# One level of Strassen on the input products of both feed-forwards, with an output stage of its own

## The chip, the cores and the metric

The kernel runs on one core of one Trainium2 chip. The metric is the device time of one launch in microseconds (us). The core has a matrix engine (TensorE, PE in the rows; its weight loads stand as PEld), a vector engine (VectorE, DVE), a scalar engine (ScalarE, ACT), GpSimd (POOL) and a queue engine (SyncE, SP) that issues the memory transfers (DMA).

## What is computed

Two layers of a streaming encoder on 1024 frames of width 1024. Each has a token mixer and then a SwiGLU feed-forward with 2816 hidden units, each with a norm and a modulation before it and a gated residual add behind it. The change touches the feed-forward alone, with the norm ahead of it:

```python
def swiglu(h, w_in, w_out):
    gate, up = jnp.split(h @ w_in, 2, axis=-1)
    return (jax.nn.silu(gate) * up) @ w_out
...
        h = modulate(rms_norm(x, ln_ffn_g[layer]), sh2, sc2)
        x = x + g2[:, None, :] * swiglu(h, ffn_w_in[layer], ffn_w_out[layer])
```

## The kernel before

Activations lie transposed: the residual `x` is eight tiles of 128 features by 1024 frames, and so is the normed input `HT`. Every large product is made of three matmuls in `mm3` (L246 to L250): each operand is held as a rounded part `hi` and a rest `lo`, and hi·hi, hi·lo and lo·hi are summed in PSUM. One matmul is 128x128 by 128x512.

`Stream` (L100 to L167) brings the weights in a planned order: a transfer of 512 KB into one of four `raw` tiles (L130), a copy to `hi` on ACT (L141) and a subtraction for `lo` on POOL (L142), into one of six `whl` slots. The pump runs at every `pipe.tick`, and generators (`ada`, `norm`, `rms`) advance by ticks too, which is how their work is set among the matmuls. `ada` (L277) is a matrix-vector product of conditioning weights: eight transfers of 512 KB and eight DVE operations (L286, L288).

`out_proj` (L1253) ends the mixer: it adds into `x` (L1266), sums squares (`stat`, L311 and L312), and at its end starts `norm` (L339) for each half of the frames. `norm` takes the row statistic through PE, DVE and POOL (`rms`, L320 to L336) and writes `hi` and `lo` of `HT` (L348 to L351).

`ffn` (L1296) walks over 22 tiles `m` of 128 hidden units. For each `m` and each half of 512 frames it makes a gate and an up product (L1321, 8 blocks of the width, 24 matmuls each), then Silu on ACT (L1326), a product (L1327) and a cast (L1328) on DVE and the rest on POOL (L1329), into `aT`. Every two tiles the output products follow (L1340): 16 groups of 6 matmuls, each added into `x` by DVE (L1342). The first three tiles are done for the first half of the frames before the second half of `HT` is needed. Five calls of `ada` for the next layer are spread over the first five blocks of layer 0. The order on each queue is set when the kernel is built, by a planner that moves an instruction ahead of earlier ones that it holds to be not yet ready.

## Time and profile before

| | us |
|---|---|
| median of 3 runs | 2644.95 (2635.11 to 2645.98) |
| the profiled execution | 2628.13 |
| its span, first to last instruction | 2626.3 |
| PE busy in it | 2535.4 |
| feed-forward of layer 0, about | 580 to 1300 |
| feed-forward of layer 1, about | 1905 to 2623 |

The profile's page gives the busy time of each engine, and the trace can be asked for stretches, groups of instructions, waits and the order in time. A matmul of 128x512 shows 0.39 us in a row because neighbours overlap; what counts is the distance between two starts.

### The profile page before, as it was taken

Reading aid. Unit: us, or ns where it says so; the run is one execution under the profiler, and the core shown is the slowest. Engines: PE = TensorE matmul, PEld = TensorE weight load, DVE = VectorE, ACT = ScalarE, POOL = GpSimd, SP = SyncE. Lnnn points to the kernel's source line nnn. Section 1 sums busy time; section 2 is a strip of 40 time slices with the busy share of each in tenths; the row PEclk is TensorE's granted clock in tenths of the full one; section 3 lists DMA queues with packets and bytes.
Section 4 is the critical chain, followed back from the end, with each engine's and each line's share of the span. In section 5 each row is a group of like instructions: output and inputs, shape, how many; then the busy total and the mean of one; then the engine's idle time right before and its main releaser. Section 6 shows DMA issues by size and latency. Waiting matters only on the chain. (4 is left out here: it accounts for less than half of the span.)

```text
span 2626.3 us, 32531 instructions
## 1 busy us (share of the span) xinstructions
PE 2535.4 (97%) x12912; PEld 2104.9 (80%) x12912; DVE 1134.9 (43%) x2058; ACT 708.9 (27%) x1293; POOL 809.5 (31%) x538
## 2 busy tenths in 40 slices
PE   6999898999999999999999999999999999999999
PEld 4898776777888888888788778887788888888887
DVE  6576563474333322222531566765632222222223
ACT  4332568322111111111232444544231111111100
POOL 3465003423222222232212143423243333333311
PEclk9999999999999999999999999999999999999999
DMA  7287764543233311111234333224311111111101
GB/s 282 92 248 211 211 179 154 184 145 108 93 113 112 113 49 48 48 49 49 87 109 145 87 104 102 68 76 156 112 65 49 49 50 49 50 50 49 49 9 64
DMA packets 145479, 267.12 MB, mean 102 GB/s; under 512 B 34416, under 2 KB 82224, under 8 KB 144560
## 3 DMA queue, kind: packets, MB, share of 16 engines
q1 hardware_dynamic: 145328, 265.05, 31.7%
q8 instruction: 102, 1.67, 0.3%
q14 instruction: 49, 0.40, 0.1%
HBM read 221.22 MB, written 45.88 MB: 102 GB/s over the span
## 5 line engine op out<-in xcount | busy, mean ns | idle before, releaser
L249 PE MATMUL mm<-HT,whl 128*128 128x512 f32 x1744 | 680.3, 390 | 4.5 <-DVE HT L351 4.4
L248 PE MATMUL mm<-HT,whl 128*128 128x512 f32 x1744 | 680.7, 391 | 1.8 <-ACT HT L350 1.5
L250 PE MATMUL mm<-HT,whl 128*128 128x512 f32 x1744 | 679.8, 390 | 0.0
L142 POOL TENSOR_TENSOR whl<-raw,whl 128x1024 fp32r<-128x1024 f32 x136 | 332.5, 2453 | 494.5 <-ACT whl L141 487.8
L249 PEld LDWEIGHTS mm<-HT,whl 128*128 128x128 f32 x1744 | 327.7, 188 | 76.4 <-DVE HT L351 6.7
L248 PEld LDWEIGHTS mm<-HT,whl 128*128 128x128 f32 x1744 | 327.7, 188 | 72.8 <-ACT HT L350 2.8
L250 PEld LDWEIGHTS mm<-HT,whl 128*128 128x128 f32 x1744 | 327.9, 188 | 68.5
L1342 DVE SCALAR_TENSOR_TENSOR x<-at,col,x 128x512 f32<-128x512 f32 x352 | 262.4, 750 | 268.6 <-PE at L250 268.4
L1327 DVE TENSOR_TENSOR sg<-sg,mm 128x512 f32<-128x512 f32 x88 | 60.4, 687 | 642.3 <-PE mm L250 642.3
L249 PE MATMUL at<-aT,wo 128*128 128x512 f32 x704 | 274.9, 390 | 1.9 <-POOL aT L1329 1.9
L250 PE MATMUL at<-aT,wo 128*128 128x512 f32 x704 | 274.8, 390 | 0.0
L248 PE MATMUL at<-aT,wo 128*128 128x512 f32 x704 | 273.1, 391 | 0.0
L248 PE MATMUL mm<-whl,HT 128*128 128x512 f32 (+1 forms) x688 | 249.5, 363 | 8.6 <-ACT HT L402 8.1
L249 PE MATMUL mm<-whl,HT 128*128 128x512 f32 (+1 forms) x688 | 244.8, 356 | 0.0
L142 POOL TENSOR_TENSOR wo<-raw,wo 128x1024 fp32r<-128x1024 f32 x44 | 107.4, 2464 | 442.4 <-ACT wo L141 442.4
L250 PE MATMUL mm<-whl,HT 128*128 128x512 f32 (+1 forms) x688 | 242.1, 357 | 0.0
L141 ACT CAST whl<-raw 128x1024 fp32r<-128x1024 f32 x154 | 161.3, 1054 | 172.3 <-PE mm L250 164.7
L1329 POOL TENSOR_TENSOR aT<-sg,aT 128x512 fp32r<-128x512 f32 x88 | 115.2, 1309 | 289.6 <-DVE aT L1328 281.9
L1326 ACT ACTIVATE sg<-mm 128x512 f32<-128x512 f32 x88 | 52.6, 598 | 518.7 <-PE mm L250 518.7
L141 ACT CAST wo<-raw 128x1024 fp32r<-128x1024 f32 x44 | 44.0, 1046 | 494.2 <-PE at L250 488.0
L248 PEld LDWEIGHTS mm<-whl,HT 128*128 128x128 f32 x688 | 138.0, 201 | 25.7 <-ACT HT L402 10.7
L249 PEld LDWEIGHTS at<-aT,wo 128*128 128x128 f32 x704 | 132.2, 188 | 30.8 <-POOL aT L1329 2.4
(295 smaller groups left out, 3193.0 us busy)
## 6 DMA issues: line engine op xcount, KB each, us to landing
raw<-in_ffn_w_in SPq DMA_DIRECT2D x88, 512.0 KB, 3.5
raw<-in_ada_w SPq DMA_DIRECT2D x80, 512.0 KB, 4.0
raw<-in_ffn_w_out SPq DMA_DIRECT2D x44, 512.0 KB, 3.4
ada<-in_ada SPq DMA_DIRECT2D x16, 512.0 KB, 10.2
qkd<-stk SPq DMA_DIRECT2D x32, 256.0 KB, 4.8
q<-qkd SPq DMA_DIRECT2D x64, 128.0 KB, 3.9
ks<-qkd SPq DMA_DIRECT2D x32, 256.0 KB, 4.3
qkd<-stk SPq DMA_DIRECT2D x16, 512.0 KB, 3.2
```

What stands on the lines that cost most here:

```text
L141: nc.scalar.copy(hi, u.raw[:, :u.n])
L142: self.low.tensor_sub(lo, u.raw[:, :u.n], hi.bitcast(F32))
L248: mm(out, lhs.hi, rhs.hi, start=start, stop=False)
L249: mm(out, lhs.hi, rhs.lo, start=False, stop=False)
L250: mm(out, lhs.lo, rhs.hi, start=False, stop=stop)
L1326: nc.scalar.activation(sg, gu[0], AF.Silu)
L1327: nc.vector.tensor_mul(sg, sg, gu[1])
L1329: nc.gpsimd.tensor_sub(a[m].lo[:, sl], sg, a[m].hi[:, sl].bitcast(F32))
L1342: nc.vector.scalar_tensor_tensor(xh, ps, self.col[layer, 5][:, n:n + 1], xh, M, A)
```

## The change

The weight of a tile `m` is taken as a 2x2 matrix of blocks (gate and up by the first and second half of the width), and the input as a 2x2 matrix (first and second half of the width by first and second half of the frames). Winograd's form of Strassen's scheme gives the four results from seven products of halves, each 4 blocks or 12 matmuls: P1 = A11·B11, P2 = A12·B21, S2·T2, S3·T3, S1·T1, A22·T4 and S4·B22, with sums S of weight blocks and sums T of input blocks.

- `Comb` builds S1 to S4 on DVE from two raw weight tiles and splits each of the seven blocks by an ACT copy and a POOL subtraction of 128x512. `raws` keeps at most two raw tiles outstanding.
- `norm_t` replaces `norm` for the second half of the frames: it forms T1 to T4 from the normed halves and splits each. T1 and B22 go into `HT`, T2 to T4 into twelve tiles `ar`, whose places the residual `x` held; so `x` is first written to memory (`xd`) in `out_proj`.
- `ffn_first` makes P1 and P2 of the first three tiles, from the first half of the frames alone.
- `ffn_in` makes the rest and combines by DVE; the activations (`hi` and `lo`) are written to memory (`ad`), 1 MB for each `m`.
- `ffn_out` is a stage of its own behind it: it loads activations back, eight tiles into `HT` and the last four elsewhere, loads `x` back from `xd`, and makes the output products, in blocks of two tiles and a last one of four. The five `ada` of layer 0 run there, one after another, a tick for every two groups.

```diff
+            some, full = (("S2", "S3"), ("S1", "A22"), ("S4",)), (("A11", "A12"), ("S2", "S3"), ("S1", "A22"), ("S4",))
+            self.win.append([st.pairs(w[m], some if m < EARLY else full, m > 0) for m in range(NH)])
...
+        while self.nd < len(self.units) and self.units[self.nd].ready and (self.units[self.nd].src is None or self.raws() < 2):
...
+class Comb:
...
+        a, b, op = {"S1": ("A21", "A22", A), "S2": ("S1", "A11", S), "S3": ("A11", "A21", S), "S4": ("A12", "S2", S)}[name]
...
+        self.stream.t.nc.vector.tensor_tensor(t, a, b, op)
...
+    def make(self, hl, names):
...
+            nc.scalar.copy(hi, z)
+            nc.gpsimd.tensor_sub(lo, z, hi.bitcast(F32))
...
+    def norm_t(self, pool, fp, ar, x, sb):
...
+        yield 1
+        yield from self.rms(pool, self.acc.pop(1))
...
+        low = [nc.gpsimd, v]
+
+        def put(dst, src):
+            nc.scalar.copy(dst.hi, src)
+            low[0].tensor_sub(dst.lo, src, dst.hi.bitcast(F32))
+            low.reverse()
+
+        for p in range(4):
+            h12, h22 = (pool.tile([P, 512], F32, tag="nf", bufs=3, name="nf") for _ in range(2))
+            for f, k in ((h12, p), (h22, p + 4)):
+                v.scalar_tensor_tensor(f, x[k][:, sl], s[:, k:k + 1], rb, M, M)
+                nc.scalar.activation(f, f, AF.Identity, bias=b[:, k:k + 1])
...
+            v.tensor_sub(t1, h12, b11.hi.bitcast(F32))
+            v.tensor_sub(t1, t1, b11.lo.bitcast(F32))
+            v.tensor_sub(t2, h22, t1)
+            put(self.T[2][p], t2)
+            v.tensor_sub(h12, h22, h12)
+            put(self.T[3][p], h12)
+            put(self.HT[:, p, sl], t1)
+            v.tensor_sub(t4, b21.hi.bitcast(F32), t2)
+            v.tensor_add(t4, t4, b21.lo.bitcast(F32))
+            put(self.T[4][p], t4)
+            put(self.HT[:, p + 4, sl], h22)
+            if p == 1:
+                yield 1
...
+            if h:
+                nc.sync.dma_start(out=self.xd[n], in_=x[n])
...
-                pipe.tick(self.norm(pool, x, h, sb))
+                pipe.tick(second() if h else self.norm(pool, x, h, sb))
...
+    def ffn_first(self, layer, fp):
...
+        for m in range(EARLY):
+            ps = self.mm_bank()
+            self.prod(ps, w[m], [self.HT[:, p, first] for p in range(4)])
...
+            pipe.tick()
+        for m in range(EARLY):
+            ps = self.mm_bank()
+            self.prod(ps, w[m][:, 512:], [self.HT[:, 4 + p, first] for p in range(4)])
+            self.gate(fp, m, self.p1[m], ps)
...
+            pipe.tick()
...
+    def ffn_in(self, layer, fp, tp):
...
+        def put(m, h, src):
+            a = tp.tile([P, 2, 512], F32R, tag="aT", bufs=3, name="aT")
+            nc.scalar.copy(a[:, 0], src)
+            nc.gpsimd.tensor_sub(a[:, 1], src, a[:, 0].bitcast(F32))
+            nc.sync.dma_start(out=self.ad[m][:, :, h * 512:h * 512 + 512], in_=a.bitcast(F32))
...
+            b = self.mm_bank()
+            self.prod(b, w.get("S2"), self.T[2])
+            u = tmp()
+            v.tensor_add(u, self.p1[m], b)
+            pipe.tick()
+            c = self.at_bank()
+            self.prod(c, w.get("S3"), self.T[3])
+            c22 = tmp()
+            v.tensor_add(c22, u, c)
...
+            d = self.at_bank()
+            self.prod(d, w.get("S1"), t1)
+            c21, c22 = c22, tmp()
+            v.tensor_add(c22, c21, d)
+            v.tensor_add(u, u, d)
...
+            e = self.at_bank()
+            self.prod(e, w.get("A22"), self.T[4])
+            v.tensor_add(c21, c21, e)
+            v.tensor_mul(c21, c21, self.sg[m])
+            put(m, 0, c21)
...
+            f = self.at_bank()
+            self.prod(f, w.get("S4"), b22)
+            v.tensor_add(u, u, f)
+            nc.scalar.activation(u, u, AF.Silu)
+            v.tensor_mul(u, u, c22)
+            put(m, 1, u)
...
+    def ffn_out(self, pool, ar, layer, x, done):
...
+                t = self.const.tile([P, 2, T], F32R, tag=f"HT{m % NK}", name="a")
+                nc.sync.dma_start(out=t.bitcast(F32), in_=self.ad[m])
...
+        for m in range(NK):
+            load(m)
...
+        for n in range(NK):
+            nc.sync.dma_start(out=x[n], in_=self.xd[n])
...
+                        self.mm3(ps, wfo[m].k(0)[:, n * P:(n + 1) * P], a[m][h], m == ms[0], m == ms[-1])
...
+                    if n % 2 or last:
                         pipe.tick()
```

## Rows read from the trace of the kernel before

**Rows 1.** Page, part 1: busy time of each engine, share, instructions.

```profile
PE 2535.4 (97%) x12912; PEld 2104.9 (80%) x12912; DVE 1134.9 (43%) x2058; ACT 708.9 (27%) x1293; POOL 809.5 (31%) x538
```

**Rows 2.** Stretches of layer 1's feed-forward: busy us (instructions) of each engine, clock, DMA.

```profile
1950.00:2250.00 300.00, 300.00 (x1321) 247.67 (x1321) 77.13 (x112) 39.84 (x46) 90.97 (x47) 1.00 0.15 51
2250.00:2590.00 340.00, 340.00 (x1497) 280.75 (x1496) 85.48 (x125) 41.42 (x49) 92.93 (x48) 1.00 0.12 38
```

**Rows 3.** PE's waits from 570 to 640 us: us in total, times, longest.

```profile
PE mm L249 <- DVE HT L351: 3.0, 5, 1.4
PE mm L248 <- ACT HT L350: 1.5, 3, 0.7
```

**Rows 4.** Page, part 5: costliest groups; busy us, mean ns, then idle before.

```profile
L1342 DVE SCALAR_TENSOR_TENSOR x<-at,col,x 128x512 f32<-128x512 f32 x352 | 262.4, 750 | 268.6 <-PE at L250 268.4
...
L249 PE MATMUL at<-aT,wo 128*128 128x512 f32 x704 | 274.9, 390 | 1.9 <-POOL aT L1329 1.9
...
L1329 POOL TENSOR_TENSOR aT<-sg,aT 128x512 fp32r<-128x512 f32 x88 | 115.2, 1309 | 289.6 <-DVE aT L1328 281.9
L1326 ACT ACTIVATE sg<-mm 128x512 f32<-128x512 f32 x88 | 52.6, 598 | 518.7 <-PE mm L250 518.7
```

**Rows 5.** DVE from 659 us, output products: start, us, line, idle before.

```profile
660.62 0.75 DVE L1342 SCALAR_TENSOR_TENSOR x<-at,col,x 128x512 f32<-128x512 f32 x1 [0.61 <-PE at L250]
661.98 0.75 DVE L1342 SCALAR_TENSOR_TENSOR x<-at,col,x 128x512 f32<-128x512 f32 x1 [0.61 <-PE at L250]
```

**Rows 6.** Groups of DVE by line and shape, columns as in rows 4.

```profile
L288 DVE SCALAR_TENSOR_TENSOR ada<-raw,scond,ada 128x1024 f32<-128x1024 f32 x70 | 98.0, 1399 | 87.3 <-DMA raw<-in_ada_w 86.9
L1327 DVE TENSOR_TENSOR sg<-sg,mm 128x512 f32<-128x512 f32 x88 | 60.4, 687 | 642.3 <-PE mm L250 642.3
L351 DVE SCALAR_TENSOR_TENSOR HT<-nf,col,HT 128x512 fp32r<-128x512 f32 x48 | 44.4, 952 | 2.3 <-ACT HT L350 1.4
...
L348 DVE SCALAR_TENSOR_TENSOR nf<-x,col,at 128x512 f32<-128x512 f32 x48 | 33.8, 740 | 4.5 <-PE at L336 4.2
```

**Rows 7.** Order in time on DVE, end of layer 1's `out_proj` and after.

```profile
1896.06 2.84 DVE L312 TENSOR_TENSOR acc<-acc,hf 128x512 f32<-128x512 f32 x1
1898.82 5.66 DVE L351 SCALAR_TENSOR_TENSOR HT<-nf,col,HT 128x512 fp32r<-128x512 f32 x2
1904.41 1.39 DVE L348 SCALAR_TENSOR_TENSOR nf<-x,col,at 128x512 f32<-128x512 f32 x2
1905.73 0.74 DVE L1266 SCALAR_TENSOR_TENSOR x<-mm,col,x 128x512 f32<-128x512 f32 x1
...
1914.51 1.76 DVE L330 TENSOR_TENSOR dgt<-ident,ss 128x512 f32<-128x512 f32 x1 [0.90 <-POOL ss L324]
```

**Rows 8.** Order in time on POOL, same stretch.

```profile
1895.94 10.81 POOL L142 TENSOR_TENSOR whl<-raw,whl 128x1024 fp32r<-128x1024 f32 x4 [12.81 <-ACT whl L141]
```

**Rows 9.** Single instructions by line: ns least, median, most; first and last start.

```profile
L351 DVE SCALAR_TENSOR_TENSOR HT<-nf,col,HT x48: 733/747/2890, 558.4 to 1936.7; 128x512 fp32r<-128x512 f32 x48
...
L312 DVE TENSOR_TENSOR acc<-acc,hf x42: 673/686/2889, 490.5 to 1907.9; 128x512 f32<-128x512 f32 x42
...
L1342 DVE SCALAR_TENSOR_TENSOR x<-at,col,x x352: 736/751/752, 644.6 to 2622.6; 128x512 f32<-128x512 f32 x176
```

**Rows 10.** Stretches of 2 us while `x` is loaded, columns as in rows 2.

```profile
484.00:486.00 2.00, 2.00 (x11) 1.65 (x10) 0.34 (x1) 0.00 (x0) 2.00 (x2) 1.00 1.02 418
```

**Rows 11.** Stretches of 2 us with a PE gap, columns as in rows 2.

```profile
1462.00:1464.00 2.00, 0.66 (x2) 0.23 (x2) 1.77 (x2) 2.00 (x6) 0.00 (x0) 0.84 0.32 88
1464.00:1466.00 2.00, 0.00 (x0) 0.00 (x0) 2.00 (x4) 1.26 (x3) 0.00 (x0) 0.50 0.35 99
...
1468.00:1470.00 2.00, 2.00 (x10) 1.78 (x9) 1.90 (x2) 1.34 (x4) 0.68 (x1) 0.50 0.09 27
1470.00:1472.00 2.00, 2.00 (x11) 1.58 (x10) 1.20 (x4) 0.66 (x2) 0.70 (x1) 0.96 0.00 0
```

More of the change, by code (lines that the diff above doesn't have):

```diff
@@ L25 @@
 FB = 2
+EARLY = 3
 EPS = 1e-6
@@ L84, in __init__ @@
         self.ready, self.act = True, None
+        self.make = self.last = None
 class Chunk:
@@ L122, in unit, with pairs @@
         return Chunk(self, [u], n)
+    def pairs(self, src, groups, first):
+        rows = [Unit(src[:, j * 1024:(j + 1) * 1024], 1024, None) for j in range(2)]
+        comb = Comb(self, rows)
+        made = [Unit(None, 1024, "whl") for _ in groups]
+        for u, names in zip(made, groups):
+            u.make = lambda hl, names=names: comb.make(hl, names)
+            for c, name in enumerate(names):
+                comb.at[name] = u, c
+        for r in rows:
+            r.last, r.ready = made[-1], first
+        self.units += rows + made
+        return comb
     def dma(self):
         u = self.units[self.nd]
+        u.issued = self.beat
+        self.nd += 1
+        if u.src is None:
+            return
         u.raw = self.t.raw()
@@ L1250, in cd_phase, with out_proj @@
             pipe.tick()
-    def out_proj(self, pool, layer, x, order, late, sb, extra):
+    def out_proj(self, pool, layer, x, order, late, sb, extra, second):
         nc, pipe = self.nc, self.pipe
@@ new lines, in arm, with prod @@
+    def arm(self, layer, fp):
+        self.stream.pool["sw"] = fp
+        for r in self.win[layer][0].rows:
+            r.ready = True
+    def prod(self, ps, w, rhs, start=True, stop=True):
+        for p in range(4):
+            self.mm3(ps, w[:, p * P:(p + 1) * P], rhs[p], start and p == 0, stop and p == 3)
+    def ffn_first(self, layer, fp):
+        nc, pipe = self.nc, self.pipe
+        first = slice(0, 512)
+        w = [c.k(0) for c in self.wfirst[layer]]
+        self.p1, self.sg = {}, {}
+        for m in range(EARLY):
+            ps = self.mm_bank()
+            self.prod(ps, w[m], [self.HT[:, p, first] for p in range(4)])
+            self.p1[m] = fp.tile([P, 512], F32, tag="p1", bufs=EARLY, name="p1")
+            nc.scalar.copy(self.p1[m], ps)
+            pipe.tick()
[3 more added lines that the diff above has]
+            self.gate(fp, m, self.p1[m], ps)
+            self.wfirst[layer][m].free()
+            pipe.tick()
@@ L1401, in build, with arena, half_layer, run @@
             k.pp = None
-    with tc.tile_pool(name="xp0", bufs=1, reuse_waits="tile") as xp:
-        x = [xp.tile([P, T], F32, name=f"x{n}") for n in range(NK)]
+    def arena(ar):
+        x = {n // 2 + n % 2 * 4: ar.tile([P, T], F32, tag="ar", bufs=12, name="x") for n in range(NK)}
+        return x
+    def half_layer(layer, ar, x, late, before, done, adas=()):
+        with tc.tile_pool(name=f"ph1{layer}", bufs=1, reuse_waits="tile") as fp:
+            with tc.tile_pool(name=f"pre{layer}", bufs=1, reuse_waits="tile") as pre:
+                k.arm(layer, fp)
+                for g in before:
+                    pipe.start(k.ada(pre, layer, g))
+                sb = [(layer, 4), (layer, 3)]
+                tail = k.norm_t(pre, fp, ar, x, sb)
+                ada = k.ada(pre, layer, 5)
+                k.out_proj(pre, layer, x, [0, 1, 2, 4, 5, 6, 7, 3], late, sb, [ada], lambda: tail)
+                k.ffn_first(layer, fp)
+                assert tail.gi_frame is None and ada.gi_frame is None
+            with tc.tile_pool(name=f"at{layer}", bufs=1, reuse_waits="tile") as tp:
+                k.ffn_in(layer, fp, tp)
+        with tc.tile_pool(name=f"ph2{layer}", bufs=1, reuse_waits="tile") as p2:
+            def run():
+                for p in adas:
+                    yield from k.ada(p2, 1, p)
+            pipe.start(run())
+            k.ffn_out(p2, ar, layer, x, lambda n, h: done(p2, n, h))
+            if layer == 0:
+                for t in range(4):
+                    pipe.tick(k.v_tile(p2, "hf", k.wdv, t))
+                    pipe.tick()
+                pipe.drain()
@@ L1435, in build @@
         k.cd_phase(dp, cp)
-    with tc.tile_pool(name="xp1", bufs=1, reuse_waits="tile") as xp:
-        x = [xp.tile([P, T], F32, name=f"x{n}") for n in range(NK)]
+    with tc.tile_pool(name="ar1", bufs=1, reuse_waits="tile") as ar:
+        x = arena(ar)
         for kk in (0, 1, 2, 4, 5, 6):
```

223 lines of the change are left out of this document (128 added, 95 removed).

## Prediction

> **What bounds the kernel now.** The page's first part comes first: PE is busy 97% of the span, no other engine half of it [rows 1]. Busy PE is not yet a bound, so the next view is stretches inside a feed-forward: PE has no idle time in 640 us and the clock is at its full 2.4 GHz [rows 2]. From the same two rows comes the price of a matmul, 640 us / 2818 = 0.227 us from start to start (the 0.39 us of a single row overlaps with its neighbour's). PE's waits around the start of layer 0's feed-forward say what could be missing there: 4.5 us in all for the norm [rows 3]. So in these two stages, 1440 us of the 2628, PE's instruction count times 0.227 us is the time, and anything that takes matmuls away pays in full unless another engine or a transfer becomes late.
>
> **What goes.** Silu runs 88 times, once for each tile and half of both layers [rows 4]; each stands for two products of 24 matmuls, so the input products are 88 x 48 = 4224. Seven products of 12 replace eight: 44 tiles x 84 = 3696. The output products stay 3 x 704 [rows 4]. 528 matmuls x 0.227 = **-120 us**. That a shorter chain of matmuls runs at the same price can be seen already: output groups of six are 1.36 us apart, 0.227 each [rows 5].
>
> **The steady input stage.** A tile now has 84 x 0.227 = 19.1 us of PE. ACT gets seven splits, a copy of P1, two Silu and two activation splits: 12 x 0.60 = 7.2 us [rows 4]. POOL gets seven weight and two activation subtractions of 128x512: 9 x 1.31 = 11.8 us [rows 4]. DVE gets seven operations with one PSUM input, 0.69 each, and six with both inputs in SBUF (four weight sums, two products): 13 x 0.69 = 9.0 us [rows 6]. All are below 19.1 us, but DVE and POOL disturb each other. Where POOL subtracted four weights in a row, at 2.70 us each, DVE operations on two SBUF inputs took 2.8 us instead of 0.69, one for each of POOL's [rows 7, 8]; with PSUM as one input 0.752 us is the most in 352 cases [rows 9]. POOL's operations will be 1.31 us, and one DVE operation beside such a one took 1.76 us [rows 7]. Six at 1.76 and seven at 0.75 make 15.8 us, still below 19.1; weights are asked for more than a tile ahead. I cost this stage at nothing; PE's 19.1 us hide it. The two transfers of activations and two of weights a tile are 2.1 MB in 19.1 us, 110 GB/s, against 418 GB/s seen [rows 10]; nothing again.
>
> **The norm of the second half**, the largest cost. Before, it was 16 DVE operations behind 30 us of PE work on three tiles. `norm_t` has 42 DVE operations: for each of four block pairs two with PSUM (L348's form) and six sums with two SBUF inputs, and 10 of the 20 subtractions for `lo` (34 with two SBUF inputs in all); POOL has the other ten. It can begin when the row statistic is spread. The last evacuation of `out_proj` starts at 1905.73 us and the diagonal is ready at 1914.51 + 1.76, 10.5 us later [rows 7]; the ticks put it behind four products, 4 x 2.72 = 10.9 us; with the small matmuls I take 12 us. On DVE there also stand the four weight sums of tile 1 and two gate sums: 38 operations with two SBUF inputs, ten with PSUM. Their price from both sides: undisturbed (L312's median [rows 9], L348's mean) 38 x 0.69 + 10 x 0.74 = 34 us; at L351's mean of 0.952, which holds POOL's disturbance in the same place [rows 6], 38 x 0.95 + 7.4 = 44 us; with every POOL operation of the stretch (ten, and five for tile 1's weights) paid in full, 34 + 15 x 1.31 = 53 us. I take 44, since L351 is the same work beside the same splits. So the last T is ready 12 + 44 = 56 us after `out_proj`. In that time PE has `ffn_first`, 72 matmuls or 16.3 us, and tile 0's 60, 13.6 us, of which the last quarter waits for the last block pair; parts of tiles 1 and 2 fit only as far as banks and weights go. 56 + 1 - 30 = 27, less 3 for such parts: PE stands 24 us in each layer, **+48 us** (ends: 12 and 45 us a layer, the latter if PE's queue also keeps the order of the program).
>
> The Trainium skill states, in SBUF — State Buffer, section "SBUF: two separate sides", that the port pair that DVE shares with GpSimd is an exclusive lock for a whole instruction, where DVE has two SBUF inputs and GpSimd reads SBUF. By that rule the norm would take the 53 us, which is a rival below. The trace agrees in kind, 2.8 us instead of 0.69, but not to the full sum: POOL's four took 10.81 us and let three DVE operations of 0.7 through in about 8.4 us of it.
>
> **The clock.** After a gap of PE around 1464 us, in which it did next to nothing for two to four us, the granted clock stood at 0.5 (1.2 GHz) from 1464 until about 1470 and then rose [rows 11]. Work in it costs twice: the price here is about 1.5 us of work lost for each long gap, **+3 us** for two.
>
> **From input to output stage.** Output needs 2.1 MB of activations (tiles 0 and 1) and `x`, 4.2 MB. The rate is 418 GB/s [rows 10], so 5 and 10 us. The loads of tiles 0 to 3 wait for `HT` 0 to 3, which the product S1·T1 of the last tile frees, 24 to 36 matmuls (5.4 to 8.2 us) before PE ends; those of 4 to 7 wait for the very last product. The first four output groups go without `x`, 5.4 us, for there are four banks; behind that PE waits for DVE and DVE for `x`. If SP issues `x` ahead of tiles 4 to 7, nothing stands; if behind them (the order of the program), `x` lands about 10 us late. SP's order is the planner's. I take 3 us a layer, **+6 us** (0 and 20).
>
> **`ada` in layer 0's output stage.** Before, one step of it came every 5.4 us, now at every second group, 2.72 us. A whole `ada` is 11 ticks, 30 us of PE. DVE has in that 22 evacuations of 0.75 and eight steps of 1.40 us [rows 6]: 27.7 us, which fits. But DVE stood 86.9 us before 70 steps for their transfers [rows 6], 1.24 us each; with these it is 37.6 us, and evacuations queue behind a waiting step. Five times 7.6 us makes 38 us as the upper end, 0 as the lower one, if the planner lets the steps slide. I take **+10 us**, since four banks take up single waits. Layer 1 has none of it.
>
> Other moves cost nothing as far as rows go: writing `x` out in `out_proj` rides beside 24-matmul groups, and the first half's norm is needed as before. The 4.5 us of old waits may go; I don't count on it.
>
> **Sum.** -120 + 48 + 3 + 6 + 10 = -53 us. On the profiled execution 2628 becomes 2575. The median of the runs shown is 16.8 us above that execution; the same difference gives 2645 - 53 = **2592 us**.
>
> **Rivals.**
> - PE fills the wait: the planner runs ready parts of tiles 1 and 2, DVE goes at its undisturbed price, 12 us a layer, and the rest hides. -120 + 24 + 3: 2552 us. For it: the planner does move matmuls ahead of ones that aren't ready. Against: three DVE operations of the old norm took 2.8 us. Chance 0.20.
> - The shared port lets nothing overlap in `norm_t`: 53 us instead of 44, so some 9 to 11 us more a layer: 2614 us. Chance 0.13.
> - `ada` binds the output stage of layer 0: 38 instead of 10, 2620 us. Chance 0.10.
> - Slower than before: the input stage becomes bound by DVE. The place is DVE's six two-SBUF operations a tile; the point is where they cost more than (19.1 - 5.3) / 6 = 2.3 us each. At 2.87 us, the most seen beside 128x1024 subtractions [rows 9], a tile takes 6 x 2.87 + 7 x 0.75 = 22.5 us, 3.4 more: 44 x 3.4 = 150 us, 2742 us. Against it: POOL's operations are half as long now. Chance 0.05.
> - The change doesn't do what it says: a product of 12 carries a cost of its own at each end, and seven cost as much as eight did. Then no gain and the stalls of 67 us: 2712 us. The even pace of groups of six speaks against it [rows 5]. Chance 0.02.
>
> My forecast has 0.50. The range of 2545 to 2632 us takes in the first three rivals and the ends of single terms; what two or three bad ends at once or the last two rivals bring is left out. A measurement of this kernel tells about 0.5% from no change, 13 us, so faster means below 2632: 0.84; within 0.5%: 0.09; slower: 0.07.
>
> **What would show it.** Each right step has a row in the profile after: 3696 input matmuls at 0.227 us and a tile every 19.1 us in the middle of `ffn_in`, PE idle near nothing there. PE's waits right after `out_proj` name `norm_t`'s DVE or POOL lines, about 24 us a layer, with the clock at 0.5 there; DVE is busy through it with two-SBUF operations of 0.9 to 1.8 us. At the change of stage PE waits some us for an activation or, through DVE, for `x`. In layer 0's output stage DVE waits for `ada` transfers, in layer 1's not. Wrong would be: a tile of more than 19.5 us in `ffn_in`; PE waiting there for weights; a stall of over 15 us at the change of stage; or PE waits behind `out_proj` of under 10 us a layer.

## The result, and the profile after

| | before | after |
|---|---|---|
| median (us) | 2642.77 (2635.11 to 2645.98, 4 runs) | 2606.67 (2605.27 to 2608.17, 4 runs) |
| the profiled execution | 2628.13 | 2606.74 |

The ratio of after to before is 0.9868, with a 95% interval from 0.9844 to 0.9891: 36 us of the median went, where 53 were forecast. The two profiled executions are only 21.4 us apart, for that of before was 14.6 us below its median. The trace accounts below are made on that pair. Line numbers below are those of after, or of the run that a row comes from.

The page's first part of after. PE has 528 instructions fewer than in [rows 1], as counted, and DVE and POOL have taken on work:

```profile
PE 2449.5 (94%) x12384; PEld 2029.7 (78%) x12384; DVE 1562.7 (60%) x2474; ACT 890.8 (34%) x1679; POOL 1091.8 (42%) x772
```

PE's busy time fell by 86 us, less than 528 x 0.227 = 120; the mean granted clock of TensorE (its share of the full 2.4 GHz) fell too, from 0.992 to 0.971. The stretches below answer to [rows 2]: two in the middle of `ffn_in`, two behind `out_proj` (columns: PE, PEld, DVE, ACT, POOL busy us with instructions, clock, DMA share, GB/s).

```profile
660.00:980.00 320.00, 320.00 (x1413) 265.00 (x1412) 205.74 (x221) 117.14 (x204) 223.60 (x152) 1.00 0.32 113
2000.00:2320.00 320.00, 320.00 (x1414) 265.05 (x1413) 204.04 (x220) 117.57 (x204) 223.73 (x153) 1.00 0.32 112
575.00:655.00 80.00, 65.03 (x249) 49.68 (x249) 72.95 (x86) 38.19 (x64) 54.46 (x36) 0.85 0.20 67
1910.00:1990.00 80.00, 64.19 (x252) 49.41 (x251) 72.23 (x90) 38.93 (x65) 52.63 (x37) 0.89 0.22 73
```

In the steady stage PE has no idle time, at 320 / 1413 = 0.2265 us a matmul and full clock; DVE is busy 0.64 of the time and POOL 0.70. Behind `out_proj` 249 and 252 matmuls stand in 80 us, and the clock is at 0.85 and 0.89 of 2.4 GHz. At 0.2265 each they are worth 56.4 and 57.1 us, so 23.6 and 22.9 us are lost. Only 15.0 and 15.8 of these are time in which PE stood; the other 8.6 and 7.1 went while it was busy, with the granted clock at its lower level (0.5 of full speed, 1.2 GHz) in parts of the stretch. Five us of it, with 13 matmuls where 22 fit:

```profile
605.00:610.00 5.00, 5.00 (x13) 3.93 (x12) 5.00 (x9) 2.64 (x5) 0.68 (x1) 0.50 0.00 0
```

The same stretches of the kernel before:

```profile
575.00:655.00 80.00, 76.89 (x342) 61.49 (x341) 38.66 (x52) 19.39 (x25) 29.75 (x16) 1.00 0.40 132
1910.00:1990.00 80.00, 80.00 (x353) 65.82 (x353) 29.12 (x43) 16.52 (x21) 26.92 (x15) 1.00 0.16 53
```

There 2.5 us were lost in layer 0 and nothing in layer 1, so the new norm costs 21 and 23 us. PE's waits in after from 570 to 660 us and from 1000 to 1300 us (us in total, times, longest) answer to [rows 3]. A row reads: the waiting engine, the tile that it writes, its line, and behind the arrow what ended the wait; `mm` and `at` are PSUM banks:

```profile
PE mm L307 <- ACT T L429: 11.7, 2, 10.0
PE at L307 <- ACT T L429: 1.1, 1, 1.1
...
PE at L353 <- DVE ada L347: 17.9, 1, 17.9
PE at L307 <- DMA a<-ad: 6.7, 1, 6.7
PE at L307 <- DVE x L1537: 2.6, 4, 0.9
PE at L379 <- DVE acc L371: 2.3, 1, 2.3
```

L429 is the cast of a T block to `hi`, the end of `norm_t`'s sums on DVE. L353 is the matrix-vector product of `ada` on PE, and `a<-ad` the load of an activation tile. The forecast had the wait at the change of stage smaller, and none of PE's own at L353.

### Where the time went, by stage

The starts of three DVE rows cut each trace into stages: the last addition into `x` of `out_proj` in each layer, and the last output addition of layer 0. The first column ends at the first of these, the last one begins at the third and ends with the last addition of the kernel. Us; first and third columns are stages that the diff leaves alone, but for the order that the planner writes.

| kernel | to `out_proj` 0 | feed-forward 0 | mixer 1 | feed-forward 1 |
|---|---|---|---|---|
| before | 574.3 | 738.4 | 593.0 | 716.9 |
| after | 577.1 | 733.6 | 600.4 | 690.1 |
| e1_ada_late | 580.1 | 723.3 | 599.4 | 688.3 |
| e2_x_behind | 580.0 | 738.2 | 601.7 | 683.0 |
| e3_early4 | 577.6 | 732.9 | 596.0 | 688.6 |
| e4_no_wait | 575.5 | 725.3 | 597.6 | 684.2 |
| e9_nowait_av | 578.0 | 727.4 | 602.5 | 686.1 |
| e6_arm_late | 574.4 | 732.8 | 596.9 | 690.6 |
| e8_two | 580.1 | 716.2 | 598.6 | 682.9 |
| e11_ada24 | 574.9 | 710.6 | 601.3 | 682.8 |
| e12_low_dve | 577.3 | 714.3 | 599.8 | 682.0 |
| e13_low_pool | 583.3 | 716.2 | 602.4 | 688.4 |
| e14_all_dve | 577.3 | 700.5 | 601.3 | 679.6 |
| e15_all_early4 | 574.7 | 707.6 | 590.0 | 681.1 |

Layer 1 gained 26.8 us and layer 0 only 4.8. The untouched stages took 10 us more in after than in the profile of before, but over the fourteen kernels they spread from 574 to 583 and from 590 to 602 us, and the profile of before is near the low end of both. The two feed-forwards together gained 31.6 us, near the 36 of the medians. A cut at a DVE row is good to a few us only: in e3_early4 and e15_all_early4 the planner puts 16 more matmuls, 3.6 us, behind the cut into feed-forward 1 than in after.

### The profile page after: what moved, and what is told of

Same layout as the page of the kernel before. It is cut to its first block, busy times and chain, and to the rows that moved or that the text cites. A ratio compares the mean times of both kernels' runs of the same rounds, so it can differ in the third digit from the quotient of the medians.

```text
span 2605.0 us, 33520 instructions
## 1 busy us (share of the span) xinstructions
PE 2449.5 (94%) x12384; PEld 2029.7 (78%) x12384; DVE 1562.7 (60%) x2474; ACT 890.8 (34%) x1679; POOL 1091.8 (42%) x772
## 5 line engine op out<-in xcount | busy, mean ns | idle before, releaser
L170 POOL TENSOR_TENSOR whl<-raw,whl 128x1024 fp32r<-128x1024 f32 x98 | 242.1, 2489 | 602.4 <-ACT whl L169 505.7
L228 POOL TENSOR_TENSOR whl<-sw,whl 128x512 fp32r<-128x512 f32 x176 | 266.7, 1526 | 67.6 <-ACT whl L227 67.6
L307 PE MATMUL at<-a,whl 128*128 128x512 f32 x704 | 279.4, 397 | 16.4 <-DMA a<-ad 13.8
L308 PE MATMUL at<-a,whl 128*128 128x512 f32 x704 | 277.4, 394 | 0.0
L309 PE MATMUL at<-a,whl 128*128 128x512 f32 x704 | 277.0, 393 | 0.0
L308 PE MATMUL mm<-HT,whl 128*128 128x512 f32 x688 | 270.1, 393 | 0.2
L307 PE MATMUL mm<-HT,whl 128*128 128x512 f32 x688 | 268.8, 393 | 1.2 <-ACT p L1420 1.1
L309 PE MATMUL mm<-HT,whl 128*128 128x512 f32 x688 | 269.2, 392 | 0.0
L228 POOL TENSOR_TENSOR whl<-raw,whl 128x512 fp32r<-128x512 f32 x120 | 178.2, 1497 | 138.8 <-ACT whl L227 138.8
L218 DVE TENSOR_TENSOR sw<-raw 128x512 f32<-128x512 f32 x88 | 144.1, 1638 | 63.0 <-POOL whl L228 61.4
L307 PEld LDWEIGHTS at<-a,whl 128*128 128x128 f32 x704 | 134.3, 191 | 47.7 <-issue 14.9
L227 ACT CAST whl<-sw 128x512 fp32r<-128x512 f32 x176 | 104.9, 620 | 165.5 <-PE at L309 111.7
L307 PEld LDWEIGHTS mm<-whl,HT 128*128 128x128 f32 x688 | 138.3, 201 | 26.9 <-ACT HT L504 11.9
L309 PEld LDWEIGHTS at<-a,whl 128*128 128x128 f32 x704 | 134.2, 191 | 28.4
L308 PEld LDWEIGHTS at<-a,whl 128*128 128x128 f32 x704 | 134.3, 191 | 27.9 <-issue 0.2
L308 PE MATMUL at<-HT,whl 128*128 128x512 f32 x384 | 151.9, 396 | 0.9 <-DVE HT L430 0.9
L307 PEld LDWEIGHTS mm<-HT,whl 128*128 128x128 f32 x688 | 130.1, 189 | 29.0 <-ACT p L1420 1.6
```

The costliest lines, as they stand in the source:

```text
L170: self.low.tensor_sub(lo, u.raw[:, :u.n], hi.bitcast(F32))
L218: self.stream.t.nc.vector.tensor_tensor(t, a, b, op)
L227: nc.scalar.copy(hi, z)
L228: nc.gpsimd.tensor_sub(lo, z, hi.bitcast(F32))
L307: mm(out, lhs.hi, rhs.hi, start=start, stop=False)
L308: mm(out, lhs.hi, rhs.lo, start=False, stop=False)
```

## The experiments

Medians, ratios to the kernel before on the same chip and their 95% intervals. e8_two joins the edits of e1_ada_late and e2_x_behind, e9_nowait_av extends e4_no_wait, and e11_ada24 to e15_all_early4 build on e8_two; the others are after with one edit.

| kernel | us | ratio |
|---|---|---|
| e1_ada_late | 2595.49 | 0.9831 [0.9809, 0.9854] |
| e2_x_behind | 2604.61 | 0.9869 [0.9845, 0.9893] |
| e3_early4 | 2600.95 | 0.9858 [0.9839, 0.9876] |
| e4_no_wait | 2590.58 | 0.9821 [0.9806, 0.9836] |
| e8_two | 2585.33 | 0.9813 [0.9794, 0.9831] |
| e9_nowait_av | 2601.07 | 0.9869 [0.9853, 0.9885] |
| e6_arm_late | 2601.15 | 0.9870 [0.9855, 0.9885] |
| e11_ada24 | 2575.61 | 0.9774 [0.9756, 0.9792] |
| e12_low_dve | 2573.91 | 0.9769 [0.9741, 0.9796] |
| e13_low_pool | 2586.34 | 0.9824 [0.9800, 0.9848] |
| e14_all_dve | 2565.17 | 0.9729 [0.9703, 0.9755] |
| e15_all_early4 | 2560.80 | 0.9727 [0.9705, 0.9749] |

### Layer 0's output stage: `ada` and the order of the loads

First what SP issued in after at the change of stage, in order of time (start, us, line, what):

```profile
1008.09 3.54 SPq L1527 DMA_DIRECT2D x<-xd  x5
1011.74 0.41 SPq L151 DMA_DIRECT2D raw<-in_ffn_w_out  x1
1012.56 1.30 SPq L1527 DMA_DIRECT2D x<-xd  x3
1014.83 4.67 SPq L1509 DMA_DIRECT2D a<-ad  x4
...
1036.92 0.33 SPq L343 DMA_DIRECT2D raw<-in_ada_w  x1
...
1049.85 1.01 SPq L1509 DMA_DIRECT2D a<-ad  x2
1053.41 2.69 SPq L343 DMA_DIRECT2D raw<-in_ada_w  x2
```

All of `x` goes ahead of the first activation tile. The first `ada` transfer is issued at 1036.92, and the bulk of them only behind two activation loads at 1049.85, for which SP had waited 6.4 us until PE was done with the tiles that they overwrite. On PE this ends in two rows (start, us, line, wait ahead of it), and the stretches of 20 us around them show the cost (the last of the four is layer 1's change of stage). DMA moves 388 to 414 GB/s in three of them:

```profile
1026.84 0.77 PE L307 MATMUL at<-a,whl 128*128 128x512 f32 x1 [6.74 <-DMA a<-ad]
...
1076.55 0.59 PE L353 MATMUL at<-ones,ada 128*128 128x1 f32 x2 [17.90 <-DVE ada L347]
```

```profile
1015.00:1035.00 20.00, 13.26 (x52) 10.54 (x51) 6.98 (x10) 3.87 (x5) 8.30 (x5) 0.83 1.02 414
1055.00:1075.00 20.00, 3.66 (x17) 2.69 (x15) 10.81 (x11) 0.00 (x0) 0.74 (x1) 0.65 0.98 388
1075.00:1095.00 20.00, 18.45 (x71) 15.32 (x72) 13.09 (x17) 0.00 (x0) 0.00 (x0) 0.75 0.65 209
2350.00:2370.00 20.00, 12.91 (x45) 10.10 (x44) 5.82 (x8) 2.89 (x5) 7.74 (x4) 0.74 1.02 409
```

52 and 45 matmuls in 20 us mean 8.2 and 9.8 us lost at the change of stage of layers 0 and 1; 88 matmuls in the 40 us from 1055 mean 20 us lost to the product of `ada`.

**e1_ada_late** lets the five `ada` begin 16 ticks later:

```diff
             def run():
+                yield 16
                 for p in adas:
```

> The five conditioning products of layer 0 start 16 ticks (two blocks of output groups) later in its output stage; all else as changed. Theory A: PE's 17.9 us stand is the first product's matvec, which sits on PE's queue ahead of output groups while its eight transfers lie behind 12 MB of activation and residual loads; started later, its transfers find free queues: 18 to 22 us less (with the half clock after the gap), about 2586 us, and no PE wait of over 4 us at that matvec. Theory B: the transfers of this stage are too many in any order, and the stand moves to a later place: under 6 us less.

The ratio fell by 0.0037, some 10 us; feed-forward 0 became 10.3 us shorter and the others hardly changed. The wait on L353 went from 17.9 to 6.3 us. What is saved is about the length by which the wait shrank, and the wait is not gone at the new place: between the two theories.

**e2_x_behind** issues the loads of `x` behind those of the first two activation tiles:

```diff
-        for n in range(NK):
-            nc.sync.dma_start(out=x[n], in_=self.xd[n])
+        with self.tc.issue_after(self.ld[1].ins):
+            for n in range(NK):
+                nc.sync.dma_start(out=x[n], in_=self.xd[n])
```

> The eight loads of the residual at the change of stage are queued behind the loads of activation tiles 0 and 1 instead of ahead of them, in both layers; all else as changed. Theory A: PE waits 6.7 and 7.1 us at the change of stage because 4.2 MB of residual travel ahead of the 2.1 MB that the first output group needs: 4 to 5 us of each wait go, with less half clock behind it, 9 to 14 us in all, about 2596 us. Theory B: the residual is now late instead and PE stands behind the vector engine after four groups: under 4 us less.

In sum nothing. But feed-forward 1 is 7.1 us shorter, as long as the wait for `a<-ad` that is gone there, and feed-forward 0 is longer. Its waits, from 1000 to 1300 us:

```profile
PE at L353 <- DVE ada L347: 23.7, 1, 23.7
PE at L307 <- DVE x L1538: 7.1, 9, 2.4
```

The wait for `a<-ad` is gone here too, but PE arrives earlier at the product of `ada`, whose transfers are no earlier, and waits 23.7 us in place of 17.9.

**e8_two** joins both edits, which tells whether they add up.

> Both edits in one kernel: the conditioning products of layer 0's output stage begin 16 ticks later, and the loads of x are issued behind those of the first two activation tiles. The late products alone took about 10 us off the changed kernel (ratio to the kernel before 0.983); the other order of the loads alone took nothing off (0.987), although layer 1's feed-forward became 7 us shorter. Theory A, what the other order gains in layer 0 is eaten by the matrix-vector product that waits for its own transfers: with that product out of the way both gains are there, 10 + 7 in layer 1 + some 5 in layer 0, 2580 to 2587 us, ratio 0.978 to 0.981. Rival B, the order of the loads is worth nothing in either layer, because PE's later work waits for x instead: ratio 0.983, as with the late products alone.

2585.3 us, ratio 0.9813: at the upper edge of theory A. Feed-forward 1 keeps the 7 us (682.9), and feed-forward 0 is 7.1 us shorter than with late `ada` alone (716.2 against 723.3). So the order of the loads is worth 7 us in each layer as soon as `ada` doesn't eat it.

**e11_ada24** puts `ada` 24 ticks behind the start, where it was 16.

> As the kernel with both edits, but the conditioning products begin 24 ticks into layer 0's output stage in place of 16. Theory A, the matrix-vector product waits only because SP and the memory transfers are full at the change of stage, and at 16 ticks something of that was left (6.3 us of PE wait): now under 2 us of it stands and the kernel is 3 to 6 us below the one with 16 ticks. Rival B, the wait belongs to the tighter pace (one step every 2.7 us against 512 KB of transfer for each) and comes back wherever the products are put: the same wait of about 6 us at a later place, and no gain over 16 ticks.

2575.6 us, 10 below e8_two, more than theory A had it: no PE wait for `ada` is left, and feed-forward 0 is down to 710.6 us, 5.6 below e8_two and 23 below after. So the stall was the place, where SP's queue and the memory transfers were full: theory A. By these runs the place is worth about 16 us (10.3 from the first 16 ticks, 5.6 from the next 8), not the whole 20. The tighter pace isn't quite free either. DVE additions into `x` queue behind `ada` steps that wait for their transfers, and PE for those additions, as two rows of after show (PE waited 0.89 us behind them):

```profile
1139.37 1.28 DVE L347 SCALAR_TENSOR_TENSOR ada<-raw,scond,ada 128x1024 f32<-128x1024 f32 x1 [1.16 <-DMA raw<-in_ada_w]
1140.58 1.41 DVE L1537 SCALAR_TENSOR_TENSOR x<-at,col,x 128x512 f32<-128x512 f32 x2
```

In e11_ada24 PE waits 7.1 us for such additions in layer 0 and 1.9 in layer 1, where no `ada` runs. In layer 0, 2.8 us of it come right at the change of stage, where `x` is now the late one:

```profile
PE at L307 <- DVE x L1538: 7.1, 6, 2.4
```

### Behind `out_proj`: what binds in the stretch of `norm_t`

**e3_early4** makes P1 and P2 of four tiles, not three, ahead of the T blocks (with three slots for weight sums where four were, so that it fits):

```diff
-EARLY = 3
+EARLY = 4
```

> Four instead of three tiles have their first two products made from the first half of the frames before the second half is ready (the weight sums get three buffers instead of four, to fit). Theory A: PE stands behind the chain of the second half's norm, whose length does not depend on this; one tile more covers 24 matmuls, 5.4 us a layer: about 11 us less, 2596 us. Theory B: the added weight splits slow the norm on the port that VectorE and GpSimd share by as much as the tile covers: under 4 us less.

PE's waits from 570 to 660 us fell from 14 to 12 us (the longest, on L429, from 10.0 to 4.7), and the last subtraction of `norm_t` came 4.2 and 6.5 us later: more work for PE ahead of the T blocks is more work for DVE too. The time can't be told from after's, which is theory B's size but not a proof of its reason. What each kernel of this part loses in the stretch is counted as for after, in 80 us around it, at 0.2265 us a matmul:

| kernel | matmuls, layers 0 and 1 | us lost |
|---|---|---|
| after | 249, 252 | 23.6, 22.9 |
| e3_early4 | 265, 267 | 20.0, 19.5 |
| e4_no_wait | 233, 232 | 27.2, 27.5 |
| e9_nowait_av | 224, 224 | 29.3, 29.3 |
| e6_arm_late | 258, 255 | 21.6, 22.2 |
| e11_ada24 | 250, 255 | 23.4, 22.2 |
| e12_low_dve | 248, 254 | 23.8, 22.5 |
| e13_low_pool | 228, 227 | 28.4, 28.6 |
| e14_all_dve | 267, 267 | 19.5, 19.5 |
| e15_all_early4 | 278, 275 | 17.0, 17.7 |

So the fourth early tile wins 3.5 us a layer in the stretch, of the 5.4 that theory A had.

**e4_no_wait** leaves out the use of the T blocks, T1 and B22: five of the seven products take normed blocks of the first half of the frames, so none of them waits for `norm_t`, which still runs.

```diff
-            self.prod(b, w.get("S2"), self.T[2])
+            self.prod(b, w.get("S2"), b11)
...
-            self.prod(f, w.get("S4"), b22)
+            self.prod(f, w.get("S4"), b21)
```

> The five products of each tile that take T1 to T4 or the second half of the input take blocks of the first half in their place, so that PE waits for nothing of the second half's norm, which still runs; the result is not the feed-forward's. Theory A: the stand behind that norm is 23 us a layer, as matmul counts of the stretches say: 42 to 48 us less, about 2561 us. Theory B: a good part of it is weights or banks that come late, and PE stands for these: under 25 us less.

The time fell by some 12 us, not by the 46 that the stretch loses, which is theory B's size, and none of the 12 comes from the stretch: PE loses 27 us a layer there, more than in after. The gain is at the change of stage. As no product reads the T tiles, their places are free for `x` at once; SP issues its loads some 405 us ahead of the first output matmul (19 in after), and no wait for `a<-ad` is left; the wait at L353 is 14.0 us, not 17.9. SP's row, the stretch, and PE's waits in it, all in layer 0:

```profile
617.30 11.32 SPq L1527 DMA_DIRECT2D x<-xd  x8
```

```profile
573.00:653.00 80.00, 56.03 (x233) 44.92 (x232) 75.77 (x85) 37.86 (x63) 53.51 (x35) 0.85 0.34 119
```

```profile
PE at L307 <- DVE nf L436: 17.0, 1, 17.0
PE at L307 <- DVE u L1474: 6.3, 1, 6.3
```

PE runs ahead and then waits 23 us for two other things: a PSUM bank that holds the spread statistic until `norm_t`'s last L436, and an evacuation (L1474) that stands behind `norm_t` on DVE.

**e9_nowait_av** leaves out the same, and puts the spread statistic into another bank.

```diff
-            rb[h] = self.at_bank()
+            rb[h] = (bank or self.at_bank)()
...
-        yield from self.rms(pool, self.acc.pop(1))
+        yield from self.rms(pool, self.acc.pop(1), self.av_bank)
```

> Leaves out the use of the T blocks, T1 and B22 as right operands, as in the run before (five products take normed blocks of the first half of the frames, so that no product waits for norm_t), and also puts the spread statistic of norm_t into the bank that attention sums used, so that none of the four banks that the products take is held until norm_t's end. Theory A, after the T blocks the held bank was the next thing that PE waited for (17 us a layer there): this run is about 25 to 35 us below that one, 2555 to 2568 us, ratio 0.968 to 0.975, and no PE wait of over 3 us stands behind out_proj. Rival B, DVE is what binds: the evacuations of the products queue behind norm_t's operations on DVE, PSUM banks fill up and PE waits for those in place of the bank: within 8 us of that run, ratio 0.979 to 0.982, with PE waiting there for evacuations on DVE for over 12 us a layer.

2601 us, 10 us more than with the bank held, 4 of them in the two feed-forwards and in this stretch (2 a layer). In layer 0 PE waits 26.9 us at once for the evacuation on DVE, and DVE's order in time shows why (start, us, line):

```profile
PE at L307 <- DVE u L1474: 26.9, 1, 26.9
```

```profile
637.31 0.68 DVE L450 TENSOR_TENSOR tn<-HT,tn 128x512 f32<-128x512 f32 x1
637.91 0.68 DVE L1469 TENSOR_TENSOR u<-p,mm 128x512 f32<-128x512 f32 x1
638.51 1.34 DVE L430 TENSOR_TENSOR T<-tn,T 128x512 fp32r<-128x512 f32 x1
```

The first evacuation of `ffn_in` (L1469) stands third from `norm_t`'s end on DVE's queue, though the last matmul of its product started at 597.50, some 40 us before. This is rival B's mechanism, though its ratio (0.979 to 0.982) was missed: with nothing to wait for in the data, PE loses more than in after. In both kernels, as in after, DVE is busy without a gap through `norm_t`, so freeing PE of the T blocks alone gains nothing. Two limits to this. In e4_no_wait and e9_nowait_av PE, running ahead, also calls for the next tile's weight sums, and `norm_t` takes 41 to 43 us in place of 33.5. And in after itself the first evacuation isn't late: there DVE waits for its product, and PE for T blocks:

```profile
632.77 0.69 DVE L1469 TENSOR_TENSOR u<-p,mm 128x512 f32<-128x512 f32 x1 [2.87 <-PE mm L309]
```

That DVE is the full engine here is shown; whether another order on its queue would let PE run was not tried.

**e6_arm_late** lets the first tile's weight sums loose at the start of `ffn_first` and not before `out_proj`.

```diff
-                k.arm(layer, fp)
+                k.stream.pool['sw'] = fp
...
         self.p1, self.sg = {}, {}
+        self.arm(layer, fp)
```

> The first tile's weight sums and splits are let loose at the start of ffn_first and not before out_proj, so that DVE's and POOL's work on them does not stand beside the statistic of the second half and the start of norm_t. Theory A, these weight operations are what made norm_t start 19 us behind out_proj in place of 12: the first norm_t operation comes 5 to 7 us earlier against the last evacuation of out_proj, the last T as much earlier, and the time falls by 8 to 14 us for both layers (ratio 0.982 to 0.984). Rival B, the work is only moved into norm_t's own stretch, where it costs the same or more, or the weights become late: no gain (0.986 to 0.989) or a loss, and PE waits name the weight slots.

No gain in the time, as rival B had it, and at most 2 us in the stretch. `norm_t` starts 17.6 and 19.2 us behind the last addition of `out_proj`, where after has 19.2 and 17.0. So this weight work is not what makes it late, or other work comes in its place; which of the two stays open.

### What a subtraction on POOL costs DVE

DVE in after, in the stretch (start, us, line), and POOL beside it:

```profile
596.35 2.05 DVE L436 SCALAR_TENSOR_TENSOR nf<-x,col,at 128x512 f32<-128x512 f32 x3
...
600.24 1.76 DVE L447 TENSOR_TENSOR nf<-nf 128x512 f32<-128x512 f32 x1
601.93 1.74 DVE L445 TENSOR_TENSOR tn<-nf,tn 128x512 f32<-128x512 f32 x1
...
604.32 0.74 DVE L436 SCALAR_TENSOR_TENSOR nf<-x,col,at 128x512 f32<-128x512 f32 x1
604.97 1.26 DVE L443 TENSOR_TENSOR tn<-nf,HT 128x512 f32<-128x512 f32 x1
...
609.83 0.68 DVE L430 TENSOR_TENSOR T<-tn,T 128x512 fp32r<-128x512 f32 x1
610.43 0.68 DVE L445 TENSOR_TENSOR tn<-nf,tn 128x512 f32<-128x512 f32 x1
...
629.22 0.68 DVE L451 TENSOR_TENSOR tn<-tn,HT 128x512 f32<-128x512 f32 x1
```

```profile
599.80 1.65 POOL L430 TENSOR_TENSOR HT<-nf,HT 128x512 fp32r<-128x512 f32 x1 [2.85 <-ACT HT L429]
601.42 1.70 POOL L430 TENSOR_TENSOR HT<-tn,HT 128x512 fp32r<-128x512 f32 x1
604.40 1.28 POOL L430 TENSOR_TENSOR T<-tn,T 128x512 fp32r<-128x512 f32 x1 [1.28 <-ACT T L429]
612.36 1.28 POOL L430 TENSOR_TENSOR T<-nf,T 128x512 fp32r<-128x512 f32 x1 [6.68 <-DVE tn L450]
```

From 606 to 612 us POOL is idle and DVE's operations on two SBUF inputs stand 0.60 us apart; beside a POOL operation one of them takes 1.25 to 1.77. From 599.8 to 622.8 eight POOL operations of together 11.6 us made eight DVE operations longer by 6.8 us in sum, 0.85 us each: more than the 0.60 that DVE would need to do the subtraction itself. The Trainium skill (SBUF — State Buffer, section "SBUF: two separate sides") calls the port pair that the two engines share an exclusive lock for a whole instruction. The trace agrees: each of the eight longer operations ends 0.54 to 0.56 us behind the end of a POOL operation (602.00 behind 601.45, 606.23 behind 605.68 above), so it got through only when POOL was done.

That DVE lost 6.8 us and not 11.6 has two causes in the same rows. Four of POOL's operations, of 1.42 to 1.72 us, began beside a DVE operation on two SBUF inputs and end 1.12 to 1.15 us behind its end: they hold a wait of their own. The other four, of 1.28 us, began beside L436, which reads PSUM and went on at its usual 0.73 to 0.74 us, so the DVE operation behind it became longer by 0.57 to 0.70 us and not by 1.1.

**e12_low_dve**, **e13_low_pool** and **e14_all_dve** build on e11_ada24, and move subtractions between the two engines:

```diff
-        low = [nc.gpsimd, v]
+        low = [v, v]
```

(`[nc.gpsimd, nc.gpsimd]` in e13_low_pool.) e14_all_dve has `[v, v]` and also does the `lo` of the first tiles' weight blocks on DVE, from `ffn_first` until tile 1:

```diff
-            nc.gpsimd.tensor_sub(lo, z, hi.bitcast(F32))
+            self.stream.low.tensor_sub(lo, z, hi.bitcast(F32))
...
+        self.stream.low = nc.vector
...
+            if m == 1:
+                self.stream.low = nc.gpsimd
```

> On the kernel with the products at 24 ticks and the x loads behind (2575.6 us, ratio 0.9774): all twenty subtractions for lo in norm_t are on DVE, none on POOL. DVE operations on two SBUF inputs stand 0.61 us apart when POOL is idle and take 1.7 to 1.78 us beside a POOL operation. Theory A, a POOL operation in norm_t costs DVE the 1.1 us by which the one beside it is longer: ten fewer give 11 us back and ten more on DVE cost 6, so norm_t, 33 us from its first operation to its last, becomes some 5 us shorter in each layer, and the time 2564 to 2570 us (ratio 0.973 to 0.9755). Rival B, the number of DVE operations counts and POOL's disturbance mostly falls elsewhere: 6 us longer in each layer, 2582 to 2590 us (0.980 to 0.983).

> The opposite edit on the same kernel: all twenty subtractions for lo in norm_t are on POOL, so that DVE has 32 operations of norm_t in place of 42. POOL has some 28 us of these in a stretch of 33 us, with a start behind DVE's first sums. Theory A (a POOL operation costs DVE 1.1 us): DVE's part stays as long, POOL's last subtraction comes later than DVE's did, 3 to 8 us more in each layer, 2580 to 2592 us (0.979 to 0.984). Rival B (the number of DVE operations counts): ten fewer take 6 us off each layer, 2560 to 2568 us (0.972 to 0.975).

> As the kernel with all lo subtractions of norm_t on DVE, and also those of the weight blocks of the first tiles (from ffn_first until tile 1), so that POOL has next to nothing in the stretch behind out_proj. Theory A: if POOL's weight subtractions disturb norm_t too, this is a few us below that kernel (0 to 6 us, 2560 to 2570); POOL's weight splits stand mostly ahead of norm_t's first operation and behind its last in this arrangement, which speaks for little. Rival B: each of these subtractions on DVE costs 0.61 us in the queue that binds and disturbs nothing less: 4 to 10 us above that kernel.

From the last addition of `out_proj` to the start of the last `lo` subtraction of `norm_t`, in layers 0 and 1: 56.4 and 54.1 us in e11_ada24, 54.6 and 52.4 with all on DVE, 57.9 and 56.8 with all on POOL, 51.7 and 51.3 with the weights' on DVE as well. In time and in the stretch, e12_low_dve can't be told from e11_ada24: the 1.7 to 1.8 us by which `norm_t`'s last subtraction comes earlier don't reach PE, and theory A's 5 us a layer are missed. e13_low_pool is some 13 us slower and loses 5 and 6 us more in the two stretches, as theory A had it. e14_all_dve is some 12 us faster than e11_ada24 by the ratios; its interval lies just below that one's. The stretch gives 3.9 and 2.7 us of that, so what gained came with the weights' subtractions, not with those of `norm_t` alone. Against e12_low_dve it is 8.7 us by the medians, more than theory A's 0 to 6; the stretch gives 4 and 3 of them. Feed-forward 1 became 3.2 us shorter, feed-forward 0 10.1: the rest there lies mostly in the output stage, which the edit doesn't touch. Plainest are the pages' DVE rows, e11_ada24 first, then e12_low_dve and e14_all_dve:

```profile
PE 2444.5 (95%) x12384; PEld 2025.7 (79%) x12384; DVE 1562.9 (61%) x2474; ACT 890.4 (35%) x1679; POOL 1095.2 (43%) x772
```

```profile
PE 2446.0 (95%) x12384; PEld 2027.4 (79%) x12384; DVE 1564.4 (61%) x2494; ACT 891.1 (35%) x1679; POOL 1066.9 (41%) x752
```

```profile
PE 2437.0 (95%) x12384; PEld 2021.7 (79%) x12384; DVE 1557.1 (61%) x2524; ACT 891.5 (35%) x1679; POOL 1020.2 (40%) x722
```

Twenty operations more cost DVE 1.5 us, and fifty more are 5.8 us less of DVE time.

**e15_all_early4** adds the fourth early tile of e3_early4 to e14_all_dve.

> On the kernel that has all lo subtractions of the stretch on DVE (2565.2 us, ratio 0.9729): P1 and P2 of four tiles in place of three are made ahead of the T blocks, with three slots for weight sums in place of four so that it fits. PE still waits there 6 us once and some 4 to 5 us in pieces in each layer, and one tile's two products are 24 matmuls, 5.4 us. Theory A, the wait is for the T blocks and PE's other work is what shortens it: 3 to 5 us less in each layer, 2555 to 2560 us (0.969 to 0.971). Rival B, DVE's queue binds: the fourth tile's weight sums, subtractions and gate sum lie on DVE ahead of norm_t's end and move it by 4 to 6 us, as they did when only this was changed (the last T 4 to 6 us later, 2 us gained in all): 2563 to 2568 us (0.972 to 0.974).

0.9727 against 0.9729: no difference, as rival B had it, though the stretch loses about 2 us a layer less. The last subtraction came 57.9 and 59.7 us behind `out_proj` in place of 51.7 and 51.3.

## Why the prediction was right or wrong

The time, 2606.7 us, lies in the range, and the forecast's case came true in its kind: 120 us go, and the rest comes back at the places named, in greater sum. By layers, in the profiled executions:

- **Layer 1.** -60 for the matmuls, +22.9 behind `out_proj`, +9.8 at the change of stage: -27.3; measured -26.8. The forecast's terms were -60 + 24 + 1.5 + 3 = -31.5.
- **Layer 0.** -60, +21, +8.2, +20 for `ada` and 4.9 us of small waits in the output stage (2.6 and 2.3 in the rows above): -5.9; measured -4.8. Forecast: -31.5 + 10 = -21.5.
- **Elsewhere.** Forecast 0, measured +10.2 between the two profiles.

Step by step:

- **What goes** was right: 528 matmuls fewer, 0.2265 us each.
- **The steady stage at no cost** was right. PE is idle nowhere in it, and the slower rival is out: a tile takes 19.0 us of PE, in which DVE is busy 12.2 and POOL 13.3.
- **The norm of the second half** came out right in sum by luck: errors in its terms cancel. `norm_t` started 19.2 and 17.0 us behind the last addition, not 12: in layer 0 the diagonal is there at 13.6 us, PE spreads it at 16.2 behind other products, and weight and gate sums stand ahead of the first operation. From there on DVE took 33.5 us, not 44: three of the four weight sums and the gate sums were paid ahead of the start, and the other 43 operations came one every 0.78 us, where the forecast's 48 in 44 us make 0.92. Its price of 0.952, L351's mean, was too high, for some of it was taken beside 128x1024 subtractions [rows 7, 8]. The last subtraction began 56.4 and 54.1 us behind `out_proj`, against 56 for the last T in the forecast, and 21 and 23 us were lost, against 24 and 1.5 for the clock. But PE stood only 15 to 16 us, and the half clock took 7 to 9. What the prediction had not seen is why PE stands: it counted matmuls that could run without T, while e4_no_wait and e9_nowait_av show that PE loses more when all could, because the evacuations queue on DVE. The rival "PE fills the wait" was shut out by that: neither operands that are ready nor a fourth early tile brought its 24 us.
- **The shared port** was right in direction. The prediction read the lock as either paid in full, 1.31 us for each POOL operation, or let through in part. The rows show operations on two SBUF inputs take turns with POOL's, and the price is 0.85 us, for PSUM operations pass. The forecast took the split of the 20 subtractions between DVE and POOL as given; it never asked whether POOL's half was worth having. It was worth nothing: e12_low_dve does without it in the same time.
- **The change of stage** was mis-sized: 3 us forecast, 8.2 and 9.8 measured (1.5 and 2.7 of it by the clock), because the step feared the wrong order. It asked whether `x` comes behind tiles 4 to 7; SP put it ahead of tiles 0 to 3, and its 4.2 MB at 410 GB/s are 10 us in front of the first activations. e2_x_behind and e8_two put the price of that order at 7 us a layer, and e4_no_wait, with `x` loaded long before, shows no loss there at all. The order that was feared, `x` behind the first tiles, costs 2 to 3.3 us of waits at that place and not 10.
- **`ada` in layer 0** failed in its main mechanism, and cost 20 us, not 10. The prediction had evacuations queue behind waiting steps on DVE, spread over the five. That happens, but small: DVE waits 22.4 us in all ahead of the 40 steps, of which at most 2.6 reach PE. In the trace the first `ada` alone costs the 20, and the engine that waits is PE: the matrix-vector product is an instruction on PE's in-order queue, which took its place before its transfers had been issued. By e1_ada_late and e11_ada24 about 16 us of it were the place; the pace that the prediction priced left 4 us of small waits in e11_ada24. The rival that has it at 38 us rested on that small mechanism.
- **The clock**: that idle PE comes back at half of 2.4 GHz was right, and its size was not: 8.6 and 7.1 us behind `out_proj`, inside the 21 and 23, where 1.5 was forecast for one gap. There were several waits one after another, and the clock fell again between them (0.50 from 605 to 610 us, 0.95 from 610 to 615, 0.50 again from 620 to 625). It falls at the change of stage and at `ada` too (0.83, 0.74 and 0.65 above), which the prediction had not counted.
- **The untouched stages** were taken at no change. The 10 us are within their spread over these kernels; what makes that spread was not tried. In the last stretch before layer 1's `norm_t`, from 1870 to 1910 us, the granted clock was 0.91 in after and 1.00 in before, and PE's order there is the planner's own for each kernel. This stays open.

That e14_all_dve gains some 6 us in feed-forward 0 outside the stretch is open too; e12_low_dve, with part of its edit, is 3.7 us longer than e11_ada24 there, so a few us of feed-forward 0 are no measure of an edit.

The two versions with `ada` late, `x` behind and the stretch's subtractions on DVE (e14_all_dve and e15_all_early4) take 2565 and 2561 us and beat both kernels, by 2.7% the one before.

## What to carry to other kernels

When matmuls are traded for vector work at a barrier, count the in-order queue of the vector engine through the barrier, with the evacuations of the very products that should fill the gap: here they stood behind the new work, whatever the data would have allowed. An operation on PE that depends on a transfer is a wait of PE: place it by when its transfer can be issued on a busy queue, not by how many ticks it has. And price an operation offloaded to POOL by what it adds to its neighbour on DVE, too.

## What the hardware showed that was not expected

- DVE operations on two SBUF inputs and subtractions on POOL took turns: in after 212 such 128x512 operations took over 0.9 us, and all of them end 0.546 to 0.555 us behind the end of a POOL operation. One subtraction on POOL cost DVE about 0.85 us (6.8 us for eight), where DVE does it in 0.60 to 0.68 us. Moving fifty of them to DVE lowered DVE's own busy time from 1562.9 to 1557.1 us. POOL waits as well: it took 1.28 us beside a DVE operation that reads PSUM, 1.42 to 1.72 where one on two SBUF inputs was under way.
- Granted clocks in 20 us around a wait of 7 us were 0.83 and 0.74, and around one of 18 us 0.65 and then 0.75: beside the wait itself 1.5 to 2.7 us were lost at each place (8.2 and 9.8 us lost for waits of 6.7 and 7.1, 20 for one of 17.9). Behind `out_proj`, with several waits in a row, it was 8.6 and 7.1 us beside 15 to 16 of waiting.
